# Mixers whose output blocks are summed head by head, in a two-layer decoder step on one Trainium2 core

## The chip, the cores and the metric

One Trainium2 chip, one of its cores. The metric is the device time of one execution in microseconds (us), median over the runs; lower is better. The engines are called by the profile's names: PE is TensorE (matrix products), DVE is VectorE, ACT is ScalarE, POOL is GpSimd, SP is SyncE, which here only issues loads. Each engine takes its instructions in the order in which the program has them.

## The reference

One step of a trunk of two layers for two groups of requests with the same weights: a prompt of 256 tokens, and 8 sequences of 4 new tokens each; together 288 tokens of 1024 features in fp32. Each layer has three sub-layers, each with a norm before, a norm behind and adaLN (shift, scale and gate per sequence, from a conditioning vector):

```python
mod = silu(c) @ ada_w + ada_b                       # 3 * 1024 per sequence
h   = rms_norm(x) * g_pre * (1 + scale) + shift
x   = x + res_w * (1 + gate) * rms_norm(sublayer(h)) * g_post
```

The sub-layers of layer 0 are: a gated feed-forward (`ffn`), the even mixer, a `ffn`; of layer 1: a `ffn`, the odd mixer, a `ffn`.

```python
# even mixer: attention beside a recurrence, one projection out
q, k, v, xg, xr = split(h @ w_in)                   # 4 + 1 + 1 + 4 + 4 blocks of 128
o_a = softmax(rope(q) rope(k)^T, window 128, sinks) v
r, i = sigmoid(xc @ wa + ba), sigmoid(xc @ wx + bx) # xc: width-4 convolution of xr
a    = exp(-8 * r * softplus(-lam));  hs_t = a_t * hs_{t-1} + sqrt(1 - a_t^2) * i_t * xc_t
y    = concat(o_a, gelu(xg) * hs) @ w_out
# odd mixer (HGRN2), 8 heads of 128
f = lb + (1 - lb) * sigmoid(fz);  k = 1 - f
S_t = diag(f_t) S_{t-1} + k_t v_t^T;  o_t = q_t S_t
y = (rms_norm(o) * gnorm * silu(g)) @ w_out
```

## The kernel before, in words

A 128x128 weight block times 288 tokens is one **product** of PE. fp32 is made of three of them: weights and activations are split into a high part (rounded to the fast fp32 form) and the rest, and `mm3` (line 337) issues high × high, high × rest, rest × high. So one **block** of 128 output features of a 1024-feature input is 8 × 3 = 24 products.

**Weights** come as units of 1 MB (8 blocks' worth is 4 units): SP loads a unit into one of `RAW = 2` buffers (`load_to`, 286); ACT copies half a unit to its high part `whi` (`split_hi`, 296), DVE subtracts to `wlo` (`split_lo`, 303). `HL = 5` halves are kept ahead. SP also loads the adaLN weights (`aw`).

**A sub-layer** is a projection in (`proj_in`, 343: 44 blocks for `ffn`, 14 for the even mixer, 32 for the odd one), a projection out to 8 blocks called y (`proj_out`, 388), and a boundary (`out_proj`, 793: `done` evicts each y block by a square on ACT, a gated copy `yg` and its square, and running sums `yss` on POOL and DVE; then roots, and the next sub-layer's `h`). `proj_in` sums its first four blocks side by side (the input half by half, as it comes); all others, and all y blocks, are summed one block after the other, so that block 0 of y needs all heads.

**The even mixer** (1050) projects xr (4 blocks), k, v, q (4), gx (4) in this order. `gates` makes the convolution and both sigmoids, `recur` the exponents, root and scan, `gated` the product with the GELU, into the tiles `m`; `att_prompt` and `att_sample` write the tiles `o`.

**The odd mixer** (1453) projects, for each pair of heads, f, q and v, and at the end the 8 gates g. A pair's recurrence is a `tree` (1291) of 7 levels: a level's products `lv` on PE, then new `Q` on DVE and `K` on POOL; behind the last level K is transposed (`ktp`), and `sm` and `o` are summed. The head is normed by `rsqrt` (539: a root on ACT with a Newton step on DVE; rows `oms`, `oiv`, `oivw`), multiplied with the gate (`os`), and split into high and rest (`o` on ACT, then on DVE).

**What sets the order.** The program is written out by a planner that runs when the kernel is built: `clk["t"]` is its guess of PE's time, `free` of the other engines', `cost` (69) prices an instruction, `avail` notes when a tile is ready. Everything beside the projections is a generator in `sides`; `run_sides` lets each go on when its inputs are ready by these guesses, and `until` fills a foreseen wait with a chunk of the **adaLN** work (64 chunks in all, each of 4 to 8 small products `ada`) or, where none is ready, with `warm` products whose result nobody reads. `drain` runs all sides to their end; both mixers call it, and load ACT's table for the roots, ahead of `proj_out`. What is guessed wrong shows on the chip as a wait, since the order is fixed by then.

Of the kernel before, what the change touches and what calls it, by code (L numbers as in the profile page):

```python
# [17 lines left out]
NT = 288  # L18
# [3 lines left out]
NB = 8  # L22
# [8 lines left out]
RAW, HL, AW = 2, 5, 3  # L31
# [6 lines left out]
MARG = 0.1  # L38
GAPS = (0.4, 0.3, 2.0, 0.2, 0.3)
# [8 lines left out]
def tile_trunk(ctx: ExitStack, tc: tile.TileContext, I: dict, O: dict):  # L48
# [14 lines left out]
    def place(e, r, c):  # L63
        free[e] = max(free[e], r) + c
        if clk["t"] < free[e] - 40:
            raise ValueError((e, clk["t"], free[e]))
        return free[e]

    def cost(e, name, n, ins, out, kw):
        if e == "V":  # L70
            return 0.195 + n / 960
        if e == "G":
            return 0.15 + n / 475
        src = "PSUM" in str(ins[0].space) if ins else False
        c = (0.2 if src else 0.25) + n / 1200
# [56 lines left out]
    bp = ctx.enter_context(tc.tile_pool(name="bp", bufs=27))  # L132
# [133 lines left out]

    def fill(t):
# [40 lines left out]
    lows = []  # L308

    def lows_to(q):  # L310
        while lows and (lows[0] <= q or avail[splits[lows[0]][0].tensor.name] <= clk["t"]):
# [19 lines left out]
    def split_some(steps):  # L331
        rest[0] -= steps
        if rest[0] <= 0 and len(splits) < min(oldest[0] + HL, nhalf):
            split_to(len(splits))
# [8 lines left out]
    def proj_in(n, hk, done, first=None):  # L343
# [35 lines left out]
        for j in range(outer, n):  # L379
            w = get_w()  # L380
# [6 lines left out]

    def proj_out(nk, hk, done, late):
        for b in range(NB):
            p = aux_ps(f"y{b}")[:, :NT]  # L390
            for k in range(nk):
# [6 lines left out]
                mm3(p, w, 128 * o, hk[k], k == 0, k == nk - 1)  # L398
                if b == NB - 1 and k == nk - 3:
# [43 lines left out]
    def ada_finish(i, g, acc):  # L443
# [8 lines left out]
        for b in range(4):  # L452
            if g:
                T.matmul(pt[:, 18 * b:18 * b + 18], lhsT=asb[:, 128 * b:128 * b + 128], rhs=foldg, start=True, stop=True)
            else:
# [10 lines left out]
                               op0=OP.add, op1=OP.mult)  # L466

# [55 lines left out]
    def ada_need(n):  # L523
# [3 lines left out]
        drain()  # L527
# [49 lines left out]
    def x_stats(prior):  # L577
# [3 lines left out]
        acc = tp.tile([128, 3, NT], F32, tag="yss", name="xss", bufs=1)  # L581
        t0 = acc.rearrange("p c t -> p (c t)")[:, :2 * NT]
# [210 lines left out]
    def out_proj(i, nk, hk):  # L793
# [3 lines left out]
        ss = tp.tile([128, 3, NT], F32, tag="yss", name="yss", bufs=1)  # L797
# [9 lines left out]
        def done(b, p):  # L807
            v, a = (dv, da) if b == NB - 1 else (V, A)
            ts = [ss[:, q, :] if b == 0 else tmp(f"ysq{q}") for q in range(ns)]
# [29 lines left out]
            if 0 < b < NB - 2:  # L839
                for q in range(ns):  # L840
                    e = V if q == 1 else G
                    e.tensor_tensor(out=ss[:, q, :], in0=ss[:, q, :], in1=ts[q], op=OP.add)
            st[b] = ts

        def late():
# [3 lines left out]
            acc = [ss[:, q, :] for q in range(ns)]  # L849
# [61 lines left out]
        table(AF.Sigmoid if i % 3 == 0 else AF.Silu)  # L911
# [33 lines left out]
    oml = cp.tile([128, 8], F32, name="oml")  # L945

# [728 lines left out]
```

## Time and profile before

| | us |
|---|---|
| median of 3 runs (lowest to highest) | 1350.29 (1349.31 to 1351.39) |
| the profiled execution | 1344.76 |
| its span, first to last instruction | 1342.5 |
| PE busy | 1284.1 (96%), 10415 instructions |
| PE's weight loads busy | 1184.7 (88%) |
| DVE busy | 792.7 (59%) |
| ACT busy | 638.0 (48%) |
| POOL busy | 181.0 (13%) |
| mean granted PE clock | 0.984 of 2.4 GHz |

The six sub-layers follow one another without overlap but for their seams: the even mixer's projection stands at about 266 to 374.5 us, its y blocks to 400 us; the odd mixer's at 875 to 1082 us, its y blocks to 1106.7 us; feed-forward stages fill the rest. A share of busy time is an average over stages, so the stages are read one by one. A busy PE need not run at full clock: the granted clock stands beside it.

### The profile page before, as it was taken

The page shows a single profiled execution, that of the slowest core. Times are in us where ns is not written, and L with a number is a line of the kernel's source. Part 1 is how long each engine was busy: PE and PEld are TensorE (multiplying, and loading weights), DVE is VectorE, ACT ScalarE, POOL GpSimd, SP SyncE. Part 2 cuts the span into 40 slices and gives each one's busy share as a digit, 9 for nine tenths or more (in the row PEclk, how much of TensorE's full clock was granted, in tenths as well). Part 3 has the DMA queues.
Part 4 walks back from the last instruction along what each step waited for, and adds up shares of the span by engine and source line. Part 5 has one row for each costly group of instructions (what it writes and reads, how often), then busy time and mean ns, then how long its engine had stood idle before and what let it go on. Part 6 is the DMA issues. An engine that isn't in the chain of part 4 may idle for free. (4 is left out here: it accounts for less than half of the span.)

```text
span 1342.5 us, 25047 instructions
## 1 busy us (share of the span) xinstructions
PE 1284.1 (96%) x10415; PEld 1184.7 (88%) x10415; DVE 792.7 (59%) x1389; ACT 638.0 (48%) x1095; POOL 181.0 (13%) x295
## 2 busy tenths in 40 slices
PE   8999999989898999999999999999989689999997
PEld 7899989868486999999799999979869688999997
DVE  4645446568765655555655545578787676655442
ACT  4644344466656444444644444464434355544442
POOL 0000001061122000010200001054333221000000
PEclk9999999989999999999999999999989799999999
DMA  9566666785756654555864464536324322544541
GB/s 378 222 261 230 214 246 220 252 330 214 300 203 249 253 188 158 198 179 182 311 233 167 174 220 158 197 126 220 115 92 158 125 67 109 202 157 164 182 157 37
DMA packets 39555, 263.46 MB, mean 196 GB/s; under 512 B 4933, under 2 KB 5509, under 8 KB 9489
## 3 DMA queue, kind: packets, MB, share of 16 engines
q1 hardware_dynamic: 35280, 249.09, 51.4%
q0 software_dynamic: 4160, 12.77, 2.7%
q8 instruction: 82, 1.34, 0.4%
q14 instruction: 33, 0.26, 0.1%
HBM read 254.69 MB, written 7.15 MB: 195 GB/s over the span
## 5 line engine op out<-in xcount | busy, mean ns | idle before, releaser
L90 PE MATMUL pj<-h,whi 128*128 128x288 f32 x3552 | 719.0, 298 | 5.1 <-ACT h L90 2.7
L90 PEld LDWEIGHTS pj<-h,whi 128*128 128x128 f32 x3552 | 568.8, 189 | 29.8 <-issue 12.7
L90 DVE TENSOR_TENSOR wlo<-raw,whi 128x1024 fp32r<-128x1024 f32 x326 | 400.1, 1236 | 231.9 <-ACT whi L90 228.0
L90 PE MATMUL pj<-h,wlo 128*128 128x288 f32 x1776 | 516.1, 295 | 3.7 <-DVE wlo L90 3.6
L90 ACT ACTIVATE whi<-raw 128x1024 fp32r<-128x1024 f32 x326 | 341.9, 1053 | 190.5 <-PE y L90 110.5
L90 PEld LDWEIGHTS pj<-h,wlo 128*128 128x128 f32 x1776 | 334.3, 189 | 5.9 <-DVE wlo L90 5.9
L90 PE MATMUL y<-mh,whi 128*128 128x288 f32 x1408 | 281.5, 296 | 0.0
L90 PEld LDWEIGHTS y<-mh,whi 128*128 128x128 f32 x1408 | 225.7, 188 | 6.3 <-ACT mh L90 2.5
L90 PE MATMUL y<-mh,wlo 128*128 128x288 f32 x704 | 207.7, 295 | 0.0
L90 POOL TENSOR_TENSOR yss<-yss,ysq 128x288 f32<-128x288 f32 x55 | 46.6, 846 | 788.7 <-ACT ysq L90 781.3
L90 PEld LDWEIGHTS y<-mh,wlo 128*128 128x128 f32 x704 | 132.5, 188 | 0.0
L90 ACT ACTIVATE mh<-fs 128x288 fp32r<-128x288 f32 x88 | 38.6, 443 | 153.5 <-DVE fs L90 153.5
L90 DVE TENSOR_TENSOR fs<-fs,pj 128x288 f32<-128x288 f32 x88 | 39.6, 454 | 85.4 <-PE pj L90 56.8
L90 ACT ACTIVATE fs<-pj 128x288 f32<-128x288 f32 x88 | 35.5, 408 | 87.9 <-PE pj L90 87.9
L90 PE MATMUL ada<-aw,cT 128*32 128x256 f32 (+1 forms) x720 | 68.1, 477 | 2.7 <-DMA aw<-in_w_ada 2.5
L90 DVE TENSOR_TENSOR mh<-fs,mh 128x288 fp32r<-128x288 f32 x88 | 42.3, 484 | 30.6 <-ACT mh L90 30.4
L90 PE MATMUL y<-o,whi 128*128 128x288 f32 x192 | 41.6, 311 | 4.2 <-ACT o L90 4.1
L90 DVE TENSOR_TENSOR yg<-y,modG 128x32 f32<-128x32 f32 x48 | 9.1, 189 | 58.8 <-ACT yg L90 58.8
L90 ACT ACTIVATE h<-hv,mod,modA 128x256 fp32r<-128x256 f32 x48 | 28.5, 593 | 30.6 <-DVE hv L90 23.0
L90 ACT ACTIVATE ysq<-y 128x288 f32<-128x288 f32 x42 | 17.2, 409 | 54.0 <-PE y L90 53.9
L90 PEld LDWEIGHTS ada<-aw,cT 128*32 128x32 f32 x720 | 18.1, 109 | 22.3 <-issue 12.8
L90 PEld LDWEIGHTS y<-o,whi 128*128 128x128 f32 x192 | 32.9, 200 | 5.2 <-ACT o L90 4.4
(288 smaller groups left out, 1099.9 us busy)
## 6 DMA issues: line engine op xcount, KB each, us to landing
raw<-in_wf_in SPq DMA_DIRECT2D x87, 1024.0 KB, 4.9
aw<-in_w_ada SPq DMA_DIRECT2D x64, 1024.0 KB, 7.0
raw<-in_wf_out SPq DMA_DIRECT2D x44, 1024.0 KB, 4.9
raw<-in_wo_in SPq DMA_DIRECT2D x16, 1024.0 KB, 5.1
awf<-in_w_ada SPq DMA_DIRECT2D x8, 1024.0 KB, 8.7
raw<-in_we_in SPq DMA_DIRECT2D x7, 1024.0 KB, 5.0
raw<-in_we_out SPq DMA_DIRECT2D x4, 1024.0 KB, 5.1
S<-in_s POOLq DMA_DIRECT2D x16, 256.0 KB, 5.4
```

The costliest lines, as they stand in the source:

```text
L90: r = f(*args, **kw)
```

## The change

- **y by heads.** In both mixers `proj_out` sums its first four blocks side by side: as soon as a head is whole (a set `whole`, filled where a head's second part is written), its 12 products for these blocks are issued, while the sides go on. Blocks 4 to 7 follow as before. Block 0 is evicted at once, blocks 1 to 3 at set places inside blocks 4 and 5. `drain` and the table load ahead of `proj_out` are gone; the table is loaded when the last head is issued, if it isn't there yet. `idle` issues `warm` products while no head is whole.
- **The even mixer** projects k, v, q first, then xr, then gx; the columns of its weights are laid out so. Its sigmoids become tanh (halves folded into the constants), which shares a table with the exponent; i's product with xc moves from POOL to DVE. The RG-LRU heads wait for recurrence, samples' attention and gx, all three.
- **F and K** of the odd mixer come from ACT (two scaled copies with a bias) rather than from DVE and POOL. In `rsqrt`, the scaled input and the square of the root come from ACT rather than from DVE.
- **Three raw buffers** for weights instead of two; 23 work tiles instead of 27; the sums `yss` are three tiles of their own.
- **The planner's guesses** are new (`cost`, 0.07 more per result), halves of weights are split only when ACT or DVE are free or the half is soon due (`LAZY`, `rush`), and an adaLN result is waited for by itself rather than by `drain`.

The core of the diff:

```diff
-RAW, HL, AW = 2, 5, 3
+RAW, HL, AW = 3, 5, 3
...
-        return free[e]
+        return free[e] + 0.07
...
-            return 0.195 + n / 960
+            return 0.125 + n / 960
         if e == "G":
-            return 0.15 + n / 475
+            return 0.1 + n / 300
         src = "PSUM" in str(ins[0].space) if ins else False
-        c = (0.2 if src else 0.25) + n / 1200
+        c = (0.14 if src else 0.19) + n / 1200
...
-    bp = ctx.enter_context(tc.tile_pool(name="bp", bufs=27))
+    bp = ctx.enter_context(tc.tile_pool(name="bp", bufs=23))
...
     def proj_out(nk, hk, done, late):
-        for b in range(NB):
+        b0 = 0
+        if nk == NB:
+            b0 = OUTER
+            ws = [get_w() for _ in range(b0)]
...
+            left = list(range(nk))
+            while left:
+                run_sides()
+                some = [k for k in left if k in whole]
+                while not some:
+                    idle(max(min(e[0] for e in sides), clk["t"] + 0.02))
+                    run_sides()
+                    some = [k for k in left if k in whole]
+                k = min(some, key=lambda q: max(ready(hk[q]), clk["t"]))
+                idle(ready(hk[k]))
+                left.remove(k)
+                if not left:
+                    table(AF.Abs_reciprocal_sqrt)
+                for b in range(b0):
+                    mm3(pp[b], ws[b], 128 * k, hk[k], len(left) == nk - 1, not left)
+                yield
+            done(0, pp[0])
+        for b in range(b0, NB):
...
+                if b0 and b < b0 + 2 and k in (1, 5) and 2 * (b - b0) + k // 4 < b0 - 1:
+                    q = 2 * (b - b0) + k // 4 + 1
+                    done(q, pp[q])
...
     def rsqrt(ms, n, name):
-        u, w = tmp(name), tmp(name + "w")
-        V.tensor_scalar(out=w, in0=ms, scalar1=1.0 / n, scalar2=EPS, op0=OP.mult, op1=OP.add)
+        u, w, s = tmp(name), tmp(name + "w"), tmp(name + "s")
         act(u, ms, AF.Abs_reciprocal_sqrt, bias=eps, scale=1.0 / n)
-        V.tensor_tensor(out=w, in0=w, in1=u, op=OP.mult)
-        V.scalar_tensor_tensor(out=w, in0=w, scalar=-0.5, in1=u, op0=OP.mult, op1=OP.mult)
+        A.activation(w, ms, AF.Identity, bias=eps, scale=1.0 / n)
+        A.activation(s, u, AF.Square)
+        V.scalar_tensor_tensor(out=w, in0=w, scalar=-0.5, in1=s, op0=OP.mult, op1=OP.mult)
...
-            act(r, pr, AF.Sigmoid, bias=ba[:, b:b + 1])
+            act(r, pr, AF.Tanh, bias=hb[:, b:b + 1], scale=0.5)
...
-                G.tensor_tensor(out=ii[b][:, :CW], in0=ii[b][:, :CW], in1=xcd[b // 2][:, b % 2, :CW], op=OP.mult)
...
+                V.scalar_tensor_tensor(out=ii[b][:, :CW], in0=ii[b][:, :CW], scalar=1.0, in1=xcd[b // 2][:, b % 2, :CW],
+                                       op0=OP.add, op1=OP.mult)
...
         drive(proj_in(14, hk, done))
-        drain()
-        table(AF.Abs_reciprocal_sqrt)
         return mix
...
-                    V.tensor_scalar(out=f, in0=f, scalar1=oml[:, hd:hd + 1], scalar2=lb[:, hd:hd + 1], op0=OP.mult, op1=OP.add)
-                    G.tensor_scalar(out=k, in0=f, scalar1=-1.0, scalar2=1.0, op0=OP.mult, op1=OP.add)
+                    A.activation(k, f, AF.Identity, scale=noml[:, hd:hd + 1], bias=oml[:, hd:hd + 1])
+                    A.activation(f, f, AF.Identity, scale=oml[:, hd:hd + 1], bias=lb[:, hd:hd + 1])
...
             yield from split_later(o, out)
+            whole.add(q)
 
         drive(proj_in(32, hk, done))
-        drain()
```

How the order moves, at three places. Over the whole program PE has the same products but for `warm` (72 rows rather than 50) and the cut of the adaLN chunks; of its 64 chunks the even mixer's projection has 9 where it had 19, the odd mixer's 12 where it had 2, and the boundary behind the even mixer 1 where it had 3.

PE, at the odd mixer's end, from the last input product on (`pj` input products, `lv` the tree's last level, `y_…<-o_…` products of one head for one output block). Before:

```order
L90 MATMUL pj_11603<-h_9380,wlo 128x288
L90 MATMUL sn_11512<-vm,ks 128x512
L90 MATMUL sn_11515<-vm,ks 128x512
L90 MATMUL lv<-Q_10893,K_10892 64x64 x4
L90 MATMUL ktp<-ident,K_10892 128x128 x4
L90 MATMUL sm<-vt,kt 128x128 x4
L90 MATMUL o<-acc,vt 128x128 x2
...
L90 MATMUL oms<-osq,ones 128x288 x2
L90 MATMUL y_11740<-o_11166,whi 128x288 x2
L90 MATMUL y_11740<-o_11166,wlo 128x288
L90 MATMUL y_11740<-o_11231,whi 128x288 x2
```

And now (66 input products stand between `lv` and `ktp`):

```order
L91 MATMUL lv<-Q_10881,K_10880 64x64 x4
L91 MATMUL pj_11572<-h_9338,whi 128x288 x2
...
L91 MATMUL pj_11668<-h_9340,wlo 128x288
L91 MATMUL ktp<-ident,K_10880 128x128 x4
L91 MATMUL y_11720<-o_11327,whi 128x288 x2
L91 MATMUL y_11720<-o_11327,wlo 128x288
L91 MATMUL y_11721<-o_11327,whi 128x288 x2
...
L91 MATMUL y_11723<-o_11327,wlo 128x288
L91 MATMUL sm<-vt,kt 128x128 x4
...
L91 MATMUL oms<-osq,ones 128x288 x2
L91 MATMUL y_11720<-o_11489,whi 128x288 x2
```

The last level has moved ahead of input products, and the products of seven heads stand around what follows it; the last head's 12 come behind 2 `warm` products.

PE, at the even mixer's end (`pvs` samples' attention, `m_…` RG-LRU heads, `o_…` attention heads). Before:

```order
L90 MATMUL ada_3854<-aw_6_3994,cT 32x512 x4
L90 MATMUL pvs<-pTss,vt 64x128
L90 MATMUL pvs<-pTss,vc_2940 64x16 x4
L90 MATMUL pvs<-pTss,vc_2941 64x16 x4
L90 MATMUL y_4057<-m_3960,whi 128x288 x2
L90 MATMUL y_4057<-m_3960,wlo 128x288
L90 MATMUL y_4057<-m_3965,whi 128x288 x2
```

And now:

```order
L91 MATMUL pvs<-pTss,vc_2938 64x16 x4
L91 MATMUL y_3889<-o_3741,whi 128x288 x2
L91 MATMUL y_3889<-o_3741,wlo 128x288
L91 MATMUL y_3890<-o_3741,whi 128x288 x2
...
L91 MATMUL y_3892<-o_3747,wlo 128x288
L91 MATMUL warm<-ones 128x128 x11
L91 MATMUL y_3889<-m_4010,whi 128x288 x2
```

The attention heads are first now, and `warm` products stand ahead of the RG-LRU heads.

ACT, at the odd mixer's end (`osq` the square that the root needs, `oiv` the root, `oivw` and `oivs` the scaled input and the root's square). Before:

```order
L90 ACTIVATE osq<-o 128x288 x2
L90 ACT_TABLE_LOAD
L90 ACTIVATE oiv<-oms,eps 128x288 x2
L90 ACTIVATE o_11602<-os_11018 128x288
L90 ACTIVATE o_11637<-os_11018 128x288
```

And now:

```order
L91 ACTIVATE osq<-o 128x288 x2
L91 ACT_TABLE_LOAD
L91 ACTIVATE oiv<-oms,eps 128x288
L91 ACTIVATE oivw<-oms,eps 128x288
L91 ACTIVATE oivs<-oiv 128x288
L91 ACTIVATE oiv<-oms,eps 128x288
L91 ACTIVATE oivw<-oms,eps 128x288
L91 ACTIVATE oivs<-oiv 128x288
L91 ACTIVATE o_11667<-os_11043 128x288
L91 ACTIVATE o_11712<-os_11043 128x288
```

The root of the pair's second head stands behind three rows of the first; before, `oiv` was alone on ACT and the others were DVE's.

## Rows read from the trace of the kernel before

**Rows 1.** The page, part 1: busy time, share of the span and instructions.

```profile
PE 1284.1 (96%) x10415; PEld 1184.7 (88%) x10415; DVE 792.7 (59%) x1389; ACT 638.0 (48%) x1095; POOL 181.0 (13%) x295
```

**Rows 2.** Chain of waits that ended last: start, length (us), engine, tile.

```profile
1082.19 0.47 DVE o L90
...
1131.98 127.17 PE pj L90 x958
```

**Rows 3.** Busy us by stage: window, length, PE, PEld, DVE, ACT, POOL, PEclk, DMA.

```profile
266.00:374.50 108.50, 97.28 (x717) 68.78 (x715) 78.34 (x162) 64.81 (x151) 30.94 (x68) 0.97 0.77 287
...
411.00:635.00 224.00, 221.27 (x1728) 214.50 (x1724) 119.74 (x146) 104.12 (x155) 16.06 (x19) 0.99 0.55 197
...
875.00:1053.60 178.60, 167.64 (x1536) 149.52 (x1532) 141.83 (x357) 83.59 (x164) 68.09 (x110) 0.98 0.39 137
1053.60:1082.20 28.60, 14.44 (x62) 12.42 (x62) 16.17 (x41) 9.17 (x19) 5.74 (x6) 0.64 0.28 97
1082.20:1106.70 24.50, 24.40 (x172) 24.02 (x176) 18.37 (x28) 15.85 (x31) 9.04 (x10) 0.93 0.26 86
```

**Rows 4.** TensorE's waits: waited for, us in total, times, longest.

```profile
PE ktp L90 <- POOL K L90: 6.7, 2, 5.6
PE krt L90 <- ACT kr L90: 5.1, 1, 5.1
PE y L90 <- ACT o L90: 4.1, 1, 4.1
PE pj L90 <- DVE wlo L90: 3.6, 4, 2.0
PE lv L90 <- DVE Q L90: 3.3, 1, 3.3
```

**Rows 5.** TensorE in order of time, odd mixer's end: start, us, operation, [wait].

```profile
1056.90 1.09 PE L90 MATMUL lv<-Q,K 128*64 128x64 f32 x8 [3.32 <-DVE Q L90]
1063.60 0.69 PE L90 MATMUL ktp<-ident,K 128*128 128x128 f32 x2 [5.61 <-POOL K L90]
...
1082.21 0.89 PE L90 MATMUL y<-o,whi 128*128 128x288 f32 x2 [4.15 <-ACT o L90]
```

**Rows 6.** POOL in order of time, odd mixer's end.

```profile
1051.63 1.26 POOL L90 TENSOR_TENSOR K<-K,Tn 128x128 f32<-128x128 f32 x2
...
1061.85 3.50 POOL L90 TENSOR_TENSOR K<-K,Tn 128x128 f32<-128x128 f32 x2
```

**Rows 7.** DVE in order of time, odd mixer's end.

```profile
1051.73 0.90 DVE L90 TENSOR_TENSOR vm<-vh,sel 128x512 fp32r<-128x512 f32 x1
...
1058.85 2.15 DVE L90 SCALAR_TENSOR_TENSOR S<-S,T,sn 128x128 f32<-128x128 f32 x8
...
1061.65 1.22 DVE L90 TENSOR_TENSOR wlo<-raw,whi 128x1024 fp32r<-128x1024 f32 x1
```

**Rows 8.** ACT in order of time, odd mixer's end.

```profile
1075.81 0.50 ACT L90 ACTIVATE oiv<-oms,eps 128x288 f32<-128x288 f32 x1
```

**Rows 9.** ACT's groups, 875 to 1107 us: count, busy us, mean ns.

```profile
L90 ACT ACTIVATE whi<-raw 128x1024 fp32r<-128x1024 f32 x40 | 42.0, 1054 | 20.2 <-DMA raw<-in_wo_in 20.2
...
L90 ACT ACTIVATE yg<-y,modG 128x256 f32<-128x256 f32 x7 | 3.3, 469 | 0.0
...
L90 ACT ACTIVATE ysq<-y 128x288 f32<-128x288 f32 x6 | 2.4, 408 | 3.8 <-PE y L90 3.7
```

**Rows 10.** TensorE's groups, 266 to 374.5 us (19 adaLN chunks).

```profile
L90 PE MATMUL ada<-aw,cT 128*32 128x512 f32 (+1 forms) x176 | 19.9, 544 | 1.8 <-DMA aw<-in_w_ada 1.7
```

**Rows 11.** Busy us from 312 to 345 us, columns as in rows 3.

```profile
312.00:345.00 33.00, 31.57 (x248) 26.89 (x249) 31.50 (x63) 20.19 (x42) 7.94 (x18) 1.00 0.46 165
```

**Rows 12.** ACT in order of time, even mixer's end.

```profile
363.33 0.60 ACT L90 ACTIVATE pTs<-pT 128x512 f32<-128x512 f32 x1 [2.10 <-PE pT L90]
363.94 1.28 ACT L90 ACT_TABLE_LOAD   x1
```

**Rows 13.** POOL's groups, 875 to 1107 us.

```profile
L90 POOL TENSOR_TENSOR yss<-yss,ysq 128x288 f32<-128x288 f32 x10 | 9.0, 904 | 25.8 <-ACT ysq L90 25.7
```

More of the change, by code (lines that the diff above doesn't have):

```diff
@@ L265, in drain, with idle @@
                 fill(min(e[0] for e in sides))
+    def idle(t):
+        while clk["t"] + KEEP < t:
+            warm(1)
+        clk["t"] = max(clk["t"], t)
     def fill(t):
@@ L332, in split_some @@
         rest[0] -= steps
-        if rest[0] <= 0 and len(splits) < min(oldest[0] + HL, nhalf):
-            split_to(len(splits))
+        n = len(splits)
+        if rest[0] <= 0 and n < min(oldest[0] + HL, nhalf):
+            if n // 2 >= len(raws) or avail[raws[n // 2].tensor.name] > clk["t"] + LAZY:
+                return
+            if n > wat[0] + rush[0] and free["A"] > clk["t"] + LAZY:
+                return
+            split_to(n)
             rest[0] = REST
@@ L379, in proj_in @@
         for j in range(outer, n):
+            rush[0] = HL if n != 2 * FB and j >= n - 4 else 1
             w = get_w()
@@ L386, in proj_in @@
             done(j, p)
+    whole = set()
     def proj_out(nk, hk, done, late):
-        for b in range(NB):
+        b0 = 0
+        if nk == NB:
+            b0 = OUTER
+            ws = [get_w() for _ in range(b0)]
+            oldest[0] = wat[0] - b0
+            rest[0] = SPARE
+            pp = [aux_ps(f"y{b}")[:, :NT] for b in range(b0)]
+            left = list(range(nk))
[16 more added lines that the diff above has]
+        for b in range(b0, NB):
+            rush[0] = HL if b >= NB - 3 else 1
             p = aux_ps(f"y{b}")[:, :NT]
@@ L526, in ada_need @@
             run_sides()
-        drain()
+        while (chunks[n - 1][0], chunks[n - 1][1] >= NC0) not in finished:
+            run_sides()
+            if (chunks[n - 1][0], chunks[n - 1][1] >= NC0) not in finished:
+                fill(max(min(e[0] for e in sides), clk["t"] + 0.02))
     def table(f):
@@ L808, in done @@
             v, a = (dv, da) if b == NB - 1 else (V, A)
-            ts = [ss[:, q, :] if b == 0 else tmp(f"ysq{q}") for q in range(ns)]
+            ts = [ss[q] if b == 0 else tmp(f"ysq{q}") for q in range(ns)]
             a.activation(ts[0], p, AF.Square)
@@ L848, in late @@
             st["y"] = aux_ps("yms")[:, :NG]
-            acc = [ss[:, q, :] for q in range(ns)]
+            acc = [ss[q] for q in range(ns)]
             sums(st["y"], acc[0], True, False)
@@ L910, in out_proj @@
         clk["busy"] = clk["end"]
-        table(AF.Sigmoid if i % 3 == 0 else AF.Silu)
+        table(AF.Exp if i == 0 else AF.Sigmoid if i == 3 else AF.Silu)
         clk["hold"] = clk["busy"]
@@ L1097, in v_side, with part @@
             G.dma_start(O["v_new"], vv[:, 128:288])
+        lacks = [3]
+        def part():
+            lacks[0] -= 1
+            if not lacks[0]:
+                whole.update(range(4, NB))
         def att_prompt(n, g0, op, last):
```

59 lines of the change are left out of this document (38 added, 21 removed).

## The prediction

> **What bounds the kernel now.** The page comes first: TensorE is busy 1284.1 of 1342.5 us, 96% [rows 1], so its idle time is 58.4 us in all, and only what takes from that counts. In the chain that ended last, one unbroken stretch of 958 products of 288 columns took 127.17 us [rows 2]: 0.1327 us each. I price covers with it.
>
> Then busy time by stage [rows 3]. The feed-forward stage from 411 to 635 us is busy 221.27 of 224.00 us: at most 2.7 us to gain. The even mixer (266 to 374.5 us) leaves 108.50 − 97.28 = 11.2 us idle, at a granted clock of 0.97 (1 is 2.4 GHz). The odd mixer's body (875 to 1053.6 us) leaves 178.60 − 167.64 = 11.0 us. The odd mixer's end (1053.6 to 1082.2 us) is the worst place: 14.44 of 28.60 us busy, at a clock of 0.64; at full clock that work is 14.44 × 0.64 = 9.2 us.
>
> Last, TensorE's waits [rows 4]: the longest are in the odd mixer, `ktp` on POOL's K 6.7, `krt` on kr 5.1, y on o 4.1, `lv` on Q 3.3 us. Its end in order of time [rows 5] shows why: the last pair's level waits 3.32 us, its transposes 5.61 us, and then, after 21 products, y waits 4.15 us for the last head. Nothing else is left to run there: every input block was through before the last pair's tree ended, and y goes block by block, so its first block needs all heads.
>
> **The odd mixer's end.** The order puts 66 input products (8.8 us) between the last level and `ktp`, and 12 products (1.6 us) of each finished head in four blocks around `ktp`, `sm`, `o` and `oms`. That adds waits: TensorE's queue is in order, so a late head holds the heads behind it too. Two chains remain. The first, last level to K: level done at 1057.99, K done at 1065.35 us, 7.4 us [rows 5, 6]; in it POOL's pair took 3.50 us and DVE's S update 2.15 us [rows 6, 7]. The 8.8 us cover it; two more 1.22 us `wlo` ahead of it would leave 1 us open. The second, root to last head: first `oiv` at 1075.81, last `o` done at 1082.66 us, 6.9 us [rows 2, 8]. Behind the last `oms` now stand three finished heads (4.8 us), the pair's first head (1.6 us) and two warm products, so about 2 us stay open, or none if ACT's square and w, two rows of about 0.41 us [rows 9] for two of DVE's 0.47 [rows 2], lie beside DVE's work. Residual with some slow clock: 4 us. At best 28.6 − 9.2 = 19.4 us goes, and 24.5 × 0.07 = 1.7 us of the next window, whose clock was 0.93 [rows 3]: 21. I take **−17 us**; ends −21, and −11 if both old waits (5.6 and 4.2 us) return in full.
>
> **The odd mixer's body.** The adaLN work is 64 chunks before and after, so I count idle time alone; a stage's length also moves by its chunks. The order has 12 chunks in the body where 2 stood; the even mixer gives up ten (19 to 9). A chunk is 19.9 / 19 = 1.05 us [rows 10]: ten are 10.5 us, as much as the idle 11.0, if they fall into the waits. Whether they do is up to the planner's guesses, which are changed as well. F and K are made on ACT, two rows of about 0.41 us, so the tree's K starts without a pass on POOL, whose levels of K end in `kr`; its reader waited 5.1 us [rows 4]. ACT grows by 32 rows, 32 × 0.42 = 13.4 us, where it was busy 83.59 of 178.60 us: hidden as long as `whi` copies stay ahead by the five weight buffers; if not, that is a rival below. I take half of the idle time: **−5.5 us**; ends 0 and −11.
>
> **The even mixer.** Attention is projected first, so its softmax runs beside the xr and gx blocks, where chunks covered it before; the tail is now four attention heads (48 products, 6.4 us), 11 warm products, then the RG-LRU heads. DVE limits part: it was busy 31.50 beside TensorE's 31.57 us in the 33 us from 312 [rows 11], and gets four more products of 312 columns (for POOL's), near 4 × 0.47 = 1.9 us. At best the idle 11.2 us and 97.28 × 0.03 = 2.9 us of clock go, less 2 us in the tail: −12. At worst only the one table load saved, 1.28 us [rows 12]: −1. I take the middle, **−7 us**, since the 11 warm products show that the order itself reckons with a hole in the tail.
>
> A load shows as a row of 1.28 us that starts 0.01 us behind the end of the activation before it [rows 12]. The Trainium skill ("ScalarE: Activation LUTs", What ACT_TABLE_LOAD costs) adds a drain of about 1.38 us to every switch. By that rule the square root's switch and the root's switch, now both in a tail, would cost 2.8 us more and the sum below would be −22; this case's rows show no such drain, and none is counted.
>
> **Evictions and the boundary.** Output blocks used to end 24 products (3.2 us) apart. Now blocks 0 to 3 end together and are handed out within blocks 4 and 5, so eight evictions fall into four blocks, 96 × 0.1327 = 12.7 us. ACT has 8 × (0.41 + 0.47 + 0.41) = 10.3 us and four `whi` of 1.05, in all 14.5 us [rows 9]; POOL 10 × 0.90 = 9.0 us [rows 13]. That is 2 us too much a mixer at most by these rows; a late `wlo` behind it may double it. I take 1.5 us each, **+3 us**; ends 0 and 8. The boundary after the even mixer keeps one chunk of three as cover: 2 × 1.05, **+2 us**; ends 0 and 4 (both mixers).
>
> **The rest.** With three raw buffers SP issues the weight loads earlier and the adaLN loads later: at most the feed-forward idle 2.7 us; **−0.5 us**, ends 0 and −2.7. Four work buffers fewer: nothing, covered as long as 23 suffice; else a writer waits for a reader, within the body's end of 0.
>
> **Sum.** −17 − 5.5 − 7 + 3 + 2 − 0.5 = −25 us on the profiled execution's 1344.76 us: 1319.8. That execution lies 5.5 us under the median of 1350.29, so the median becomes **1325 us**. Ends: −21 − 11 − 12 − 2.7 = −46.7 (1304), and −11 − 1 + 8 + 4 = 0 (1350).
>
> **Rivals.** *The chains still end the odd mixer.* POOL's pair took 1.26 us beside one `vm` and 3.50 us beside two `wlo`, of which the first is shown [rows 6, 7], and K's last level stays on POOL, behind the state's transfers. If `ktp` and the last head are as late as now and the chunks miss the body's waits: −11, body 0, even mixer −4, the rest +4.5, together −10.5: **1340 us**. For it: the guesses were wrong by 5.6 us here before. Against it: 8.8 us of cover where there was none. Chance 0.15.
>
> The Trainium skill ("GPSIMD Engine Reference", Specifications) says that GpSimd shares its SBUF interfaces with VectorE and contends with instructions of two SBUF inputs. The 3.50 us pair beside `wlo` agrees; `vm` has two such inputs as well and the pair beside it took 1.26 us, so the rule does not give the size.
>
> *ACT becomes the bound: slower.* The mechanism is ACT's queue, in order like TensorE's. If each of the 32 added activations in the odd body holds up a `whi` by its own time and TensorE waits for the `wlo` behind it, the body loses 13.4 us; with the crowded evictions at 8 and the boundary at 4 that is 25.4 us. The last head's `o` is ACT's too and then comes as late as before, so the end gives 11: −11 − 7 − 0.5 = −18.5 us. Together +6.9: **1357 us**. It decides from 18.5 us of delay on. For it: TensorE already waits 3.6 us for `wlo` [rows 4]. Against it: ACT is busy under half of the body [rows 3]. Chance 0.06.
>
> *All waits go:* the lower end, **1304 us**. Against it: DVE is full at 312 to 345 us. Chance 0.08.
>
> *It doesn't do what it says*, the time staying at 1350 us: the order shows the moves, so 0.02.
>
> **How the numbers follow.** The forecast has 0.69, the rivals 0.15, 0.06, 0.08 and 0.02. A measurement of this kernel can tell about 0.2%, 2.7 us, from no change. The range, 1308 to 1343 us, holds the forecast and the first rival but for its last 0.04, and leaves out the other three: 0.2. Faster: 0.69 + 0.08 + 0.11 of the first rival = 0.88; same: its last 0.04 and 0.02 = 0.06; slower: 0.06.
>
> **What would show it.** In the changed profile: a gap before `ktp` of at most 1 us and before the last head of at most 3 us, at a clock above 0.9; K and o gone from the top of TensorE's waits; the odd body at about 178.6 + 10.5 − 5.5 = 184 us and the even mixer at about 108.5 − 10.5 − 7 = 91 us, each up to its last level or head; on ACT the evictions of two blocks within one block's time in the y stretches. The prediction is wrong if `ktp` or the last head waits over 4 us, if `krt` still waits 5 us, if blocks 4 to 7 of y wait for `wlo`, or if a feed-forward stage changes by over 2.7 us.

## The result, and where the time went

The changed kernel took **1319.96 us** (1319.83 to 1320.0, 3 runs) against 1350.29: ratio 0.9775, 95% interval 0.9753 to 0.9797. That is 30 us less; the forecast was 25, 1325 us in a range from 1308 to 1343. The sum came out nearly right. Its reasons did not, as the runs below show: without the heads' products, to which the forecast laid most of the gain, the changed kernel is no slower; the planner's guesses are worth some 19 us; and parts that it priced at nothing or at half a microsecond cost 11 and 34 us when they are undone.

The page of the changed kernel, part 1 ([rows 1] before):

```profile
PE 1283.1 (97%) x10419; PEld 1186.7 (90%) x10419; DVE 786.6 (60%) x1373; ACT 650.1 (49%) x1124; POOL 167.8 (13%) x283
```

PE's busy time is the same (1283.1 for 1284.1 us); the span fell from 1342.5 to 1318.2 us, so idle time from 58.4 to 35.1 us. The mean granted clock rose from 0.984 to 0.993.

Busy time by stage of the changed kernel, columns as in [rows 3]: the even mixer up to its first head of y, its end with y, and the feed-forward stage behind; the odd mixer's body up to its last input product, its end up to the last head, and the rest of its y.

```profile
265.60:354.10 88.50, 84.92 (x622) 65.91 (x620) 70.17 (x144) 55.55 (x141) 20.52 (x48) 0.98 0.65 242
354.10:388.00 33.90, 32.20 (x232) 29.36 (x232) 23.84 (x46) 22.94 (x42) 14.79 (x26) 0.95 0.29 111
400.00:617.60 217.60, 216.99 (x1654) 211.57 (x1654) 123.14 (x147) 106.17 (x159) 16.41 (x21) 1.00 0.55 196
860.40:1043.90 183.50, 179.74 (x1634) 155.91 (x1634) 140.66 (x363) 100.87 (x196) 65.62 (x106) 0.98 0.54 195
1043.90:1061.50 17.60, 17.41 (x127) 16.37 (x125) 6.63 (x15) 7.82 (x18) 1.12 (x2) 1.00 0.26 101
1061.50:1081.30 19.80, 15.21 (x101) 14.88 (x101) 15.81 (x22) 13.22 (x26) 9.08 (x10) 0.91 0.30 105
```

The odd mixer's end, 14.44 of 28.60 us busy at a clock of 0.64 before, is now 17.41 of 17.60 us at full clock, with the y products of seven heads among it. But the last stretch of y, dense before, leaves 4.6 us of 19.8 idle. TensorE's waits say where ([rows 4] before):

```profile
PE pj L91 <- DVE wlo L91: 7.8, 4, 3.8
PE y L91 <- DVE wlo L91: 6.2, 2, 4.5
...
PE y L91 <- ACT o L91: 0.3, 1, 0.3
```

The waits for K, kr and Q are gone from the list, and that for o has fallen from 4.1 to 0.3 us; `wlo` heads it, 7.8 us ahead of input products and 6.2 us ahead of y. In order of time at the odd mixer's end, TensorE ([rows 5] before):

```profile
1032.47 1.12 PE L91 MATMUL lv<-Q,K 128*64 128x64 f32 x8
...
1043.91 0.60 PE L91 MATMUL ktp<-ident,K 128*128 128x128 f32 x4
...
1061.55 0.40 PE L91 MATMUL y<-o,whi 128*128 128x288 f32 x1 [0.15 <-DVE o L91]
...
1071.26 0.61 PE L91 MATMUL y<-o,wlo 128*128 128x288 f32 x1 [4.54 <-DVE wlo L91]
```

The last level comes at 1032.47 us, `ktp` at 1043.91 without a wait, the last head after 0.15 us; and then, within the four remaining blocks, y waits 4.54 us for `wlo`.

A stage's length moves with the adaLN chunks that it holds, so I read both for all kernels, in the profiled execution of each. Each stage runs here from the first `yms` row of one boundary (`yms` are the products that sum the squares of y) to that of the next. In brackets stand the chunks in it, 1.05 us each, counted from PE's rows (8 rows of 512 columns or 16 of 256 are one chunk; with the 12 or 13 ahead of the first boundary every kernel comes to 64). The last column is the number of input products that the order has between the last pair's last level and its `ktp`.

| kernel | median us | even | ffn | ffn | odd | ffn | products |
|---|---|---|---|---|---|---|---|
| before | 1350.3 | 143.8 (23) | 234.8 (11) | 230.3 (12) | 242.2 (6) | 221.6 | 0 |
| changed | 1320.0 | 132.3 (14) | 229.6 (9) | 231.8 (12) | 231.9 (16) | 222.3 | 66 |
| changed again (e9) | 1319.0 | 131.8 (14) | 229.6 (9) | 231.0 (12) | 231.5 (16) | 221.9 | 66 |
| y by block (e1) | 1318.4 | 137.9 (16) | 226.5 (9) | 228.2 (10) | 229.1 (16) | 221.9 | 66 |
| heads in even only (e11) | 1316.8 | 134.2 (14) | 229.7 (9) | 231.0 (12) | 229.2 (16) | 221.8 | 66 |
| old guesses (e6) | 1339.4 | 139.6 (14) | 232.0 (9) | 232.0 (12) | 239.2 (16) | 224.1 | 0 |
| y by block, old guesses (e10) | 1333.2 | 142.5 (19) | 227.0 (8) | 229.5 (11) | 241.3 (13) | 221.6 | 0 |
| no laziness (e12) | 1330.5 | 135.2 (14) | 231.9 (9) | 231.8 (12) | 234.8 (16) | 224.1 | 24 |
| roots on DVE (e4) | 1330.7 | 133.4 (14) | 229.6 (9) | 231.1 (12) | 243.6 (16) | 222.7 | 45 |
| F, K on DVE, POOL (e3) | 1319.5 | 133.6 (14) | 229.6 (9) | 231.7 (12) | 231.8 (16) | 221.7 | 30 |
| xr first (e2) | 1337.7 | 151.4 (14) | 229.2 (9) | 231.6 (12) | 230.7 (16) | 221.4 | 66 |
| two raw buffers (e5) | 1353.9 | 136.6 (14) | 245.1 (9) | 231.8 (12) | 229.8 (16) | 236.6 | 39 |
| `wlo` ahead (e7) | 1327.0 | 133.3 (14) | 234.3 (9) | 231.2 (12) | 234.0 (16) | 221.8 | 66 |
| one eviction a block (e8) | 1323.5 | 132.5 (14) | 233.4 (9) | 231.0 (12) | 227.4 (16) | 227.5 | 66 |

From before to changed, chunks taken out: even −11.5 + 9 × 1.05 = −2 us; odd −10.3 − 10 × 1.05 = −21 us; the three feed-forward stages together −3.1 + 2 × 1.05 = −1 us. So nearly all of the 24 us between the two profiled executions is in the odd mixer.

How far a stage repeats: two executions of the changed kernel (changed and e9) differ by 0.3 us in the odd stage and by 0.8 us at most. But e11's even stage, with the same products in the same order, is 2.4 us longer than e9's, at a mean granted clock of 0.949 rather than 0.974. So I read no effect from 2 us in one even stage.

### The profile page after: what moved, and what is told of

Same layout as the page of the kernel before. It is cut to its first block, busy times and chain, and to the rows that moved or that the text cites. A ratio compares the mean times of both kernels' runs of the same rounds, so it can differ in the third digit from the quotient of the medians.

```text
span 1318.2 us, 25060 instructions
## 1 busy us (share of the span) xinstructions
PE 1283.1 (97%) x10419; PEld 1186.7 (90%) x10419; DVE 786.6 (60%) x1373; ACT 650.1 (49%) x1124; POOL 167.8 (13%) x283
## 4 chain that ended last, share of the span: by engine, by line
PE 88%; DVE 5%; DMA 3%; ACT 3%; issue 1%; POOL 0%; SPq 0%; DVEq 0%; ACTq 0%
PE pj L91 52%; PE y L91 23%; PE ada L91 4%; DMA aw<-in_w_ada 2%; PE lv L91 2%; DVE wlo L91 1%; PE o L91 1%; ACT whi L91 1%; PE adaT L91 1%; DMA raw<-in_wf_in 1%; DVE yg L91 1%; DMA awf<-in_w_ada 1%; PE pv L91 0%; PE dg L91 0%; PE warm L91 0%
## 5 line engine op out<-in xcount | busy, mean ns | idle before, releaser
L91 PEld LDWEIGHTS y<-mh,wlo 128*128 128x128 f32 x704 | 132.5, 188 | 0.0
```

Source lines behind the costliest of these rows:

```text
L91: r = f(*args, **kw)
```

## Experiments

The kernels ran in three groups; those of a group share a chip and its runs of the kernel before (medians 1354.58 for e1 to e4, 1352.07 for e5 to e8, 1349.71 for e9 to e12). A median is compared with one of the same group; across groups I go by the ratios to the kernel before, with their intervals. My theory: the head-wise sum closes the odd mixer's end, the rest is small. The rivals: the planner's guesses do it, or the work that was moved to ACT.

**e1: y block by block again**, the rest of the change kept.

```diff
-        if nk == NB:
+        if nk == 0:
             b0 = OUTER
...
         drive(proj_in(14, hk, done))
+        drain()
+        table(AF.Abs_reciprocal_sqrt)
...
         drive(proj_in(32, hk, done))
+        drain()
+        table(AF.Abs_reciprocal_sqrt)
```

> The changed kernel, but y is summed block by block in both mixers again, with all sides run out and the table loaded ahead of it; all else stays changed. If the head-wise sum is the main part of the gain: the odd end gets its holes back and the time rises by 12 to 20 us, to 1332 to 1340. If the planner's new guesses are the main part: it rises by under 6 us, since the tree of the last pair then ends early anyway.

Measured: 1318.38 us (1315.79 to 1319.47, 4 runs), ratio 0.9728 (0.9707 to 0.9750). Not slower at all. TensorE at the odd mixer's end:

```profile
1030.94 1.12 PE L91 MATMUL lv<-Q,K 128*64 128x64 f32 x8
...
1041.23 0.60 PE L91 MATMUL ktp<-ident,K 128*128 128x128 f32 x4
...
1053.04 1.10 PE L91 MATMUL y<-o,whi 128*128 128x288 f32 x2 [3.25 <-ACT o L91]
```

`ktp` has no wait here either: the last level stands 66 input products ahead of it in this kernel too. Only the last head's wait is back, 3.25 us, and the 4.5 us wait for `wlo` in y is gone in exchange. My theory falls for this kernel: in the odd mixer the heads' products cover 3 us and cost 4.5. By stage, chunks taken out: the odd one is 2.7 us shorter by block, the feed-forward stage behind the even mixer 3.1 us shorter, the even one 3.5 us longer (at a clock of 0.938 for 0.974).

**e2: the even mixer projects xr first**, as before (the columns of its weights too).

```diff
-            if 6 <= j < 10:
-                j -= 6
+            if j < 4:
...
-            elif j == 0:
+            elif j == 4:
                 side(rope(p, kk, cos, sin, lambda: G.dma_start(O["k_new"], kk[:, 128:288])))
...
```

> The changed kernel, but the even mixer projects xr first, then k, v, q, then gx, as before. If the new order of projections carries the even mixer's share (some 2 us net so far by the two traces): 1321 to 1326, with the attention's chain last in its end instead of the recurrence's. If the order is worth nothing because either chain leaves a hole ahead of y: 1318 to 1321. Below 1318 if the hole of about 5 us ahead of the RG-LRU heads was made by the new order.

Measured: 1337.70 us (1336.03 to 1341.27), ratio 0.9882 (0.9853 to 0.9910): 18 us above the changed kernel (and above e3, on the same chip), and 12 beyond my highest case. The even stage grew from 132 to 151 us. PE in order of time:

```profile
348.79 0.95 PE L91 MATMUL scs<-kc,qs 64*32 64x256 f32 x8 [3.29 <-POOL qs L91]
...
362.14 6.07 PE L91 MATMUL warm<-ones 128*128 128x128 f32 x52
369.45 0.40 PE L91 MATMUL y<-m,whi 128*128 128x288 f32 x1 [1.24 <-ACT m L91]
```

The last input product ends at 345.5 us, and the first head of y starts at 369.4: 24 us in which TensorE has attention's own small products and 26 `warm` ones, 6.07 us for 2.62 us in the changed kernel. Since the RG-LRU heads still wait for the samples' attention here, all eight heads are late together, and summing by heads has nothing to sum. So 18 us is the price of the old order within the changed kernel, not of the order alone.

**e3: F on DVE and K on POOL again.**

```diff
-                    A.activation(k, f, AF.Identity, scale=noml[:, hd:hd + 1], bias=oml[:, hd:hd + 1])
-                    A.activation(f, f, AF.Identity, scale=oml[:, hd:hd + 1], bias=lb[:, hd:hd + 1])
+                    V.tensor_scalar(out=f, in0=f, scalar1=oml[:, hd:hd + 1], scalar2=lb[:, hd:hd + 1], op0=OP.mult, op1=OP.add)
+                    G.tensor_scalar(out=k, in0=f, scalar1=-1.0, scalar2=1.0, op0=OP.mult, op1=OP.add)
```

> The changed kernel, but F is made on DVE and K on POOL again. If the removed wait of krt (5.1 us before) came from K's pass on POOL: the time rises by 3 to 6 us, to 1323 to 1326, and the wait shows again. If it came from the planner's guesses: within 1.5 us of 1320.

Measured: 1319.48 us (1318.30 to 1322.00), ratio 0.9742 (0.9720 to 0.9763): no difference, and no wait of `krt` among the longest. Waits for POOL's K are back (`lv` 2.5 us, `ktp` 2.2 us), but the odd stage is as long as in the changed kernel. That move is worth nothing here.

**e4: the roots' input and product on DVE again.**

```diff
-        A.activation(w, ms, AF.Identity, bias=eps, scale=1.0 / n)
-        A.activation(s, u, AF.Square)
-        V.scalar_tensor_tensor(out=w, in0=w, scalar=-0.5, in1=s, op0=OP.mult, op1=OP.mult)
+        V.tensor_tensor(out=w, in0=w, in1=u, op=OP.mult)
+        V.scalar_tensor_tensor(out=w, in0=w, scalar=-0.5, in1=u, op0=OP.mult, op1=OP.mult)
```

> The changed kernel, but the scaled input and the product with the root are DVE's again. If the roots are covered by the products of finished heads: within 1 us of 1320. If the last pair's chain is bare: 1321 to 1323.

Measured: 1330.66 us (1329.56 to 1332.71), ratio 0.9824 (0.9803 to 0.9844): 11 us more than the changed kernel, and than e3 on the same chip, and 8 beyond my upper case, nearly all in the odd stage (243.6 us). The head of its list of waits:

```profile
PE y L91 <- DVE wlo L91: 6.6, 3, 4.5
PE krt L91 <- ACT kr L91: 3.9, 1, 3.9
```

The two groups that came back to DVE, 850 to 1094 us:

```profile
L91 DVE TENSOR_TENSOR oivw<-oivw,oiv 128x288 f32<-128x288 f32 x8 | 3.8, 476 | 7.3 <-ACT oiv L91 7.3
...
L91 DVE TENSOR_SCALAR oivw<-oms 128x288 f32<-128x288 f32 x8 | 3.7, 458 | 9.3 <-PE oms L91 9.3
```

7.5 us of DVE's work bring back a wait of 3.9 us for kr, and the last level stands 45 instead of 66 products ahead. Whether the work itself costs that, or only where the planner then puts the tree's steps, these rows don't part.

**e5: two raw buffers.**

```diff
-RAW, HL, AW = 3, 5, 3
+RAW, HL, AW = 2, 5, 3
```

> The changed kernel with two raw buffers for weights instead of three. If the third buffer is worth nothing, as forecast: 1319 to 1322. If it carries the loads over the gaps: 1323 or more, with waits of whi for DMA. If it holds up the adaLN loads (waits of ada for aw came to 1.1 us at one boundary): below 1319.

Measured: 1353.92 us (1352.11 to 1357.24, 10 runs), ratio 1.0013 (0.9993 to 1.0033): all that the change won is gone. Of the 34 us (32 by the ratios) two waits are 27.5, one behind each mixer (TensorE's waits):

```profile
PE pj L91 <- DVE wlo L91: 20.3, 9, 13.5
PE pj L91 <- ACT whi L91: 14.0, 1, 14.0
```

ACT in order of time, from the end of the even mixer's y to the stage behind:

```profile
388.45 2.00 ACT L91 ACTIVATE whi<-raw 128x1024 fp32r<-128x1024 f32 x2
...
414.78 1.28 ACT L91 ACT_TABLE_LOAD   x1
416.08 0.20 ACT L91 ACTIVATE tab<-eps 128x1 f32<-128x1 f32 x1
416.19 1.04 ACT L91 ACTIVATE whi<-raw 128x1024 fp32r<-128x1024 f32 x1
```

From 390.45 to 416.19 us ACT splits no weights; the next half stands behind all of the boundary's rows and a table load, and TensorE waits 14.01 us for it. By the code the lazy rule does this: it splits no half whose load is not yet issued or is guessed late, and with two buffers a unit's load waits until the unit two before it is split, rather than three before. The kernel before had two buffers, split without that rule, and had no such wait. A run with two buffers and without the rule was not made, so the rule's part is argued.

**e6: the planner's old guesses** (prices, no 0.07 us, no lazy splitting).

```diff
-        return free[e] + 0.07
+        return free[e]
...
-            return 0.125 + n / 960
+            return 0.195 + n / 960
...
-                        (free["V"] <= clk["t"] + LAZY or lows[0] <= wat[0] + rush[0])):
...
-            if n > wat[0] + rush[0] and free["A"] > clk["t"] + LAZY:
-                return
```

> The changed kernel with the planner's old prices, without the 0.07 us per result and without the rule that splits weights only when ACT or DVE are free. If the guesses carry a good part of the gain: 1326 to 1335, with waits in the odd body back. If the head-wise sum carries nearly all: 1319 to 1324.

Measured: 1339.41 us (1338.03 to 1343.53), ratio 0.9908 (0.9877 to 0.9940): 20 us more, beyond the upper case. By stage, with the same chunks as e9: 7.8 us in the even stage, 7.6 in the odd one, 5.7 in the three feed-forward stages. The last level of the last pair stands behind all input products again; 12 products of a head are all that covers `ktp`, and they cover it, for it has no wait:

```profile
1059.42 0.60 PE L91 MATMUL ktp<-ident,K 128*128 128x128 f32 x4
```

**e7: the halves of blocks 4 and 5 split ahead of the evictions.**

```diff
+            oldest[0] = wat[0]
+            split_to(wat[0] + 1)
+            lows_to(wat[0] + 1)
             done(0, pp[0])
```

> The changed kernel, but when the last head is summed the weight halves of blocks 4 and 5 are split on ACT and DVE ahead of the first eviction. If the waits of y for wlo (4.5 and 1.7 us) come from DVE's order, where wlo stands behind three evictions: these waits go and the time falls by 3 to 6 us, to 1314 to 1317. If DVE and ACT are simply full there: the wait moves to block 6, and the time stays within 1 us of 1320.

Measured: 1326.96 us (1326.29 to 1329.72), ratio 0.9815 (0.9786 to 0.9844) beside 0.9775 and 0.9767 for the changed kernel: some 5 us slower by the ratios, though the intervals overlap, and not faster, as I had expected. The wait didn't go, it moved from block 5 to block 6 and grew, and DVE is late at the even mixer's boundary. TensorE in order of time:

```profile
381.91 0.40 PE L91 MATMUL y<-m,wlo 128*128 128x288 f32 x1 [2.98 <-DVE wlo L91]
...
405.99 2.83 PE L91 MATMUL warm<-ones 128*128 128x128 f32 x8 [3.65 <-DVE yg L91]
...
1080.55 0.61 PE L91 MATMUL y<-o,wlo 128*128 128x288 f32 x1 [5.91 <-DVE wlo L91]
```

**e8: one eviction in each of blocks 4, 5 and 6.**

```diff
-                if b0 and b < b0 + 2 and k in (1, 5) and 2 * (b - b0) + k // 4 < b0 - 1:
-                    q = 2 * (b - b0) + k // 4 + 1
+                if b0 and b < NB - 1 and k == 3:
+                    q = b - b0 + 1
```

> The changed kernel, but blocks 1 to 3 are evicted one in each of blocks 4, 5 and 6, instead of within 4 and 5. If the crowding of evictions makes the waits for wlo: they shrink and the time falls by 2 to 5 us, to 1315 to 1318. If the later evictions only move into the boundary: 1319 to 1323.

Measured: 1323.54 us (1322.46 to 1323.78), ratio 0.9784 (0.9757 to 0.9812): no gain; the 3.5 us above the changed kernel's median are 1 to 2 by the ratios, within the intervals. The wait in y shrank from 4.54 to 1.59 us and the odd stage from 231.8 to 227.4, but the feed-forward stages behind both mixers, boundary included, grew by 3.8 and 5.2 us. TensorE in order of time, in y and in the second boundary:

```profile
1070.85 0.40 PE L91 MATMUL y<-o,wlo 128*128 128x288 f32 x1 [1.59 <-DVE wlo L91]
...
1083.97 0.71 PE L91 MATMUL xyms<-ysq,mean 128*32 128x72 f32 x16 [2.35 <-DVE ysq L91]
```

Busy time in 13 us of that boundary:

```profile
1079.00:1092.00 13.00, 8.98 (x99) 7.11 (x98) 11.01 (x25) 5.29 (x12) 1.63 (x2) 0.68 0.64 231
```

And in the changed kernel:

```profile
1081.00:1094.00 13.00, 11.41 (x140) 9.70 (x139) 11.13 (x28) 5.80 (x14) 1.29 (x4) 1.00 0.48 171
```

TensorE waits 2.35 us for the last `ysq`, and its mean granted clock in the 13 us is 0.68 rather than 1.00. So the evictions' price is paid in y or in the boundary; at the odd mixer it is some 4 to 5 us by these stages either way.

**e9: the changed kernel once more**, as the measure for the last group.

> The changed kernel itself, as the measure for the other three on this chip: 1318 to 1324. Where its ratio to the kernel before lies beside that of the run with y by block (0.9728), the two differ by chips alone; at 0.9775 again, y by block would be the faster one.

Measured: 1319.03 us (1317.85 to 1321.11), ratio 0.9767 (0.9728 to 0.9805). That lies beside 0.9775 and not beside 0.9728, so by the rule that I had set y by block is the faster one, by some 5 us. The intervals overlap, so this is likely and not settled.

**e10: e1 and e6 together**, y by block and the old guesses.

> The changed kernel with y block by block and with the planner's old prices and no lazy splitting: both parts undone. If the two are two cures for the same hole at the odd mixer's end (each hardly missed while the other is there): 8 to 15 us slower than the kernel with old guesses alone (1339), its odd end back at about 50 us or more. If the guesses alone set the end, whichever way y is summed: 1336 to 1343. If the head-wise sum is only a loss: below 1336.

Measured: 1333.23 us (1331.09 to 1336.56), ratio 0.9871 (0.9822 to 0.9920). The hole is back, as before the change. TensorE in order of time:

```profile
1051.63 1.12 PE L91 MATMUL lv<-Q,K 128*64 128x64 f32 x8
1058.26 1.11 PE L91 MATMUL ktp<-ident,K 128*128 128x128 f32 x4 [5.52 <-POOL K L91]
...
1071.86 0.90 PE L91 MATMUL y<-o,whi 128*128 128x288 f32 x2 [3.19 <-ACT o L91]
```

DVE in the same stretch:

```profile
1052.53 2.35 DVE L91 TENSOR_TENSOR wlo<-raw,whi 128x1024 fp32r<-128x1024 f32 x2
1054.80 2.14 DVE L91 SCALAR_TENSOR_TENSOR S<-S,T,sn 128x128 f32<-128x128 f32 x8
```

Behind the last level DVE does two `wlo` (2.35 us) and the S update (2.14 us), as S stands ahead there in [rows 7]; `ktp` waits 5.52 us. And yet this kernel is not slower than e6, which sums by heads (its ratio lies lower, though the intervals overlap). The four kernels e9, e1, e6, e10 read as a square, across groups: by medians the new guesses bring 15 us by block and 20 by heads, by the ratios 19 in both rows; and y by block lies some 5 us lower in both rows, with intervals that overlap. So by the total heads bring nothing in either row.

The stages tell more. In the odd stage the heads do close the hole where the old guesses leave it: `ktp` has no wait in e6, and its odd stage is 5.3 us shorter than here, chunks taken out. The four other stages of e6 are together 10 us longer, and that is why the total hides it. In the changed kernel the guesses have closed the hole already, and the heads' products make the odd stage 2.4 to 2.7 us longer (e9 and changed beside e1). In the odd stage the two are cures for the same hole: the guesses bring 15 us there by block, 8 by heads.

And this kernel, with neither heads nor new guesses, is already 17 us below the kernel before (0.9871). So over half of the 30 us comes from other parts of the change; in the odd stage it is 8 of the 21 us, chunks taken out. Which parts, no run shows: the order, the roots and the buffer were undone only beside heads and new guesses.

**e11: by heads in the even mixer alone.**

```diff
-        if nk == NB:
+        if nk == NB and NB not in whole:
             b0 = OUTER
...
         drive(proj_in(32, hk, done))
+        drain()
+        table(AF.Abs_reciprocal_sqrt)
+        whole.add(NB)
```

> The changed kernel, with y by heads in the even mixer alone and by block in the odd one. By the stage times of the runs so far (odd stage 3 us shorter by block, even stage 2 us shorter by heads): 2 to 5 us faster than the changed kernel on the same chip. If the adaLN chunks move elsewhere and cost what is won: within 1.5 us of it.

Measured: 1316.80 us (1316.05 to 1317.85), ratio 0.9749 (0.9712 to 0.9786), beside 1319.03 for the changed kernel on the same chip. It is the fastest of its group and 2.2 us is what the stages promised, but the two ratios' intervals overlap, so the gain is likely and not settled. Its odd stage has 229.2 us for 231.5; but the profiled executions took 1317.85 us both, the even stage of this one being 2.4 us longer at the lower clock told of above.

**e12: the new prices without the lazy splitting.**

```diff
-                        (free["V"] <= clk["t"] + LAZY or lows[0] <= wat[0] + rush[0])):
...
-            if n // 2 >= len(raws) or avail[raws[n // 2].tensor.name] > clk["t"] + LAZY:
-                return
-            if n > wat[0] + rush[0] and free["A"] > clk["t"] + LAZY:
-                return
```

> The changed kernel with the new prices, but weight halves split as early as before (no LAZY rule, no rush). If the prices carry the gain of the guesses: within 3 us of the changed kernel. If the late splitting carries it: 12 to 20 us slower, like the kernel with all old guesses, since wlo stands ahead of the tree's steps on DVE again.

Measured: 1330.51 us (1329.68 to 1332.46), ratio 0.9852 (0.9814 to 0.9890), 11.5 us more than e9. So a good half of the guesses' 20 us is the lazy splitting, the rest the prices. The 12 us between the profiled executions are spread: 3.4 in the even stage, 3.3 in the odd one, 5.3 in the feed-forward stages. At the odd mixer's end the last column of the table shows what moves: 0 products between the last level and `ktp` with the old guesses, 24 with the new prices, 66 with the lazy splitting as well.

I had expected that a `wlo` which is not made early no longer stands ahead of a tree's step on DVE. At the last level that isn't so. The changed kernel has three `wlo` there where e10 has two (DVE, then POOL's last K):

```profile
1031.47 3.48 DVE L91 TENSOR_TENSOR wlo<-raw,whi 128x1024 fp32r<-128x1024 f32 x3
```

```profile
1037.88 0.92 POOL L91 TENSOR_TENSOR K<-K,Tn 128x128 f32<-128x128 f32 x2
```

K is done 5.2 us behind the level's end there, and 5.8 us in e10: about the same chain, with 66 products under it rather than none. Why the level itself comes earlier is not shown. The number of products alone doesn't set the time: e3 has 30, its `ktp` waits 2.2 us, and it takes no longer.

## Why the prediction was right in its sum and wrong in its parts

**The sum, −25.** On the profiled execution, for which it was worked out, it is almost exact: 1344.76 to 1319.96 us, −24.8. The median missed by 5 us because I added 5.5: the kernel before had its profiled execution that far under its median, the changed kernel has not. That the sum is exact is luck in part. The odd mixer came out, the even mixer brought 5 us less than forecast, and the boundaries and feed-forward stages some 4 more.

**The odd mixer's end, −17, and its body, −5.5.** Right in size: the body has 183.5 us for 178.6 with ten chunks more, −5.6; end and y together have 37.4 us for 53.1 ([rows 3] before), −15.7, where −17 and half of the evictions' +3 made −15.5. The first chain went as forecast: 66 products cover it, 7.4 us of chain before, no wait now. What failed is the cause. I read the 66 products from the order and counted them to the heads' summing; e1 and e10 show that they are there without it and gone with the old guesses. The heads would have closed that hole under the old guesses, with 12 products (e6); here they found it closed. The second chain, roots to last head, was to be covered by the heads: it is (0.15 us), and without them costs 3.25 us (e1).

**F, K and the roots on ACT: nothing.** Right for F and K (e3: 0), wrong for the roots (e4: 11 us, 11.8 in the odd stage). I priced the roots by the last pair alone, where they are covered; that on DVE they stand ahead of the tree's steps in all four pairs is my reading of e4, not shown. ACT's rows were also longer than the 0.41 us taken from a plain row. ACT's groups of the changed kernel, 850 to 1082 us:

```profile
L91 ACT ACTIVATE F<-F,lb,oml 128x288 f32<-128x288 f32 x8 | 5.0, 629 | 0.3
L91 ACT ACTIVATE K<-F,oml,noml 128x288 f32<-128x288 f32 x8 | 5.0, 629 | 0.3
...
L91 ACT ACTIVATE oivw<-oms,eps 128x288 f32<-128x288 f32 x8 | 4.0, 502 | 0.0
...
L91 ACT ACTIVATE F<-pj 128x288 f32<-128x288 f32 x8 | 3.2, 405 | 3.3 <-PE pj L91 3.3
```

**The even mixer, −7.** Measured −2 for the stage with the boundary ahead of it, and −0.5 for projection and y alone (122.4 us for 133.4 with ten chunks fewer), 1.65 us of evictions' wait in it. The hole in its end is larger than the 2 us I left: between the first attention head at 354.15 us and the first RG-LRU head at 364.72 us, 10.6 us, TensorE has 48 products, 6.4 us at full clock; 2.62 us are `warm`, and the granted clock was 1.2 GHz from 354.3 to 357.7 us. ACT's two table loads stand in that chain (ACT in order of time):

```profile
354.38 1.28 ACT L91 ACT_TABLE_LOAD   x1
355.68 1.52 ACT L91 ACTIVATE rr<-rr,quarter 128x624 f32<-128x624 f32 x2
357.22 1.28 ACT L91 ACT_TABLE_LOAD   x1
358.51 1.26 ACT L91 ACTIVATE gx<-gx 128x576 f32<-128x576 f32 x2
```

Both are rows of 1.28 us with the next row 0.02 us or less behind them; the drain that the Trainium skill ("ScalarE: Activation LUTs", What ACT_TABLE_LOAD costs) adds to a switch doesn't show here either. The order of the projections, which I priced inside this term, is worth 18 us in the changed kernel: with attention last the hole is 24 us (e2).

**Evictions, +3.** The waits for `wlo` in y are 4.54 and 1.65 us, 6.2 in all, within the ends 0 and 8 and twice what I took. The prediction named waits of blocks 4 to 7 for `wlo` as a sign of being wrong, and in this term it was. The place in DVE's queue shows why; POOL's rows beside it stand below it:

```profile
1068.44 1.03 DVE L91 TENSOR_TENSOR yss<-yss,ysq 128x288 f32<-128x288 f32 x1
1069.40 1.81 DVE L91 TENSOR_TENSOR wlo<-raw,whi 128x1024 fp32r<-128x1024 f32 x1
...
1071.83 0.46 DVE L91 TENSOR_TENSOR yss<-yss,ysq 128x288 f32<-128x288 f32 x1
```

```profile
1068.37 1.75 POOL L91 TENSOR_TENSOR yss<-yss,ysq 128x288 f32<-128x288 f32 x2 [0.28 <-ACT ysq L91]
1071.99 0.96 POOL L91 TENSOR_TENSOR yss<-yss,ysq 128x288 f32<-128x288 f32 x1 [1.87 <-ACT ysq L91]
```

The four weight halves of blocks 0 to 3 are all held until the last head is summed, and the fifth is block 4's; so block 5's `whi` can be made only then (ACT, from 1063.51 us), and its `wlo` stands behind three evictions' rows on DVE. In these rows the engine that starts first keeps its time: a `yss` on DVE takes 1.03 us where POOL's pair of its own sums started 0.07 us ahead of it, and 0.46 us where it starts 0.16 us ahead of POOL's, which then takes 0.96 us. The `wlo` that starts within POOL's pair took 1.81 us; that of [rows 7] started 0.20 us ahead of POOL's pair [rows 6], took 1.22 us, and the pair took 3.50. This is the sharing that the Trainium skill ("GPSIMD Engine Reference", Specifications) states for VectorE's instructions of two SBUF inputs, and these rows agree.

**The boundary after the even mixer, +2.** That feed-forward stage became 5.2 us shorter, 3 of them beyond its two chunks, where I had taken it as longer. It changed by over 2.7 us, and this was the second of the prediction's signs of being wrong that came. The cost itself is there: with y by block and the same nine chunks the stage is 3.1 us shorter still (e1). What else in the change made it shorter is not shown.

**The third buffer, −0.5 with −2.7 as its end.** This term failed by far: without it the kernel loses 34 us (e5). I priced it against the waits of the kernel before, where weights were split early; in the changed kernel the lazy rule, by the code, needs it.

**The planner's guesses** had no term of their own but stood inside the body's −5.5. They are worth 15 to 20 us by medians, 19 by the ratios (e6, e10), 8 of them in the odd stage where y is summed by heads. The parts don't add: undone one by one, guesses (20), order (18), roots (11) and buffer (34) cost 83 us when added up, and the whole change brought 30.

The rivals: the chains no longer end the odd mixer; ACT didn't become the bound, though it was busy 100.87 of 183.50 us in the odd body; 35 us of waits are left, so not all went.

## What to carry to other kernels

When a change has many parts and the order is set by a planner, read from the order what covers a wait, and then ask which part of the change put it there: the order of the kernel with that part undone answers it. Two parts can be cures for the same hole, so undo them one by one and both together, and read the square stage by stage: a total can hide that a part wins in one stage what it loses in others. A part whose waits look cheap in the old program can be what another part stands on, so price it in the changed program. And a sum that comes out right does not show that its terms were.

## What the runs showed that I had not expected

A scaled copy with scale and bias from tiles took 629 ns on ACT for 288 columns, where the square of such a tile without them took 450 ns. Within a wait of 2.35 us in a thin boundary the granted clock fell to 1.2 GHz, at 1083.7 us, and stayed there for 13.7 us (e8); the changed kernel kept 2.4 GHz in such a stretch (11.41 of 13 us busy, for 8.98). And one `whi` that was placed behind a boundary's rows in ACT's queue cost 14.0 us of TensorE's time (e5), and a `wlo` behind the other mixer 13.5 us.
